# Projecting memory's keys and values first, three jobs with 512 columns, and other rules in the list schedule

## The chip, the cores and the metric

The kernel runs on one core of one Trainium2 chip. The metric is the device time of one execution in microseconds (us). Three runs of the kernel before took 517.40, 517.46 and 520.27 us, the median is 517.46. The profile is one further execution, which took 516.72 us, with a span of 514.9 us from its first to its last instruction.

## The reference

One decoder layer on 512 tokens of width 1024. Four groups of heads work side by side on one projection of the normed input, and their outputs, gated, go through one output projection:

```
h = RMSNorm_pre(x)
cols = h @ w_in       # q, k, v of four groups, and z
A: MoBA block attention, 8 heads x 64     B: NSA attention (compressed, selected, window), 8 heads x 64
C: retention, 4 heads, key 64, value 128
D: cross-attention into 256 memory tokens, 4 heads x 128; keys and values = RMSNorm(mem) @ w_mem_kv
o = concat(A, B, C, D) * silu(z)
out = x + RMSNorm_post(o @ w_out)
```

Everything is fp32. With 512 tokens, MoBA and the selected and window branches of NSA come down to causal attention over all tokens.

## The kernel before, in words

**Products.** Each fp32 operand is split into a high part H, which TensorE takes in its fast fp32r format, and a low part L = operand - H. A product is three matmuls, H·H, H·L and L·H. For the weights, a piece of 512 KB (128 partitions x 1024 columns) is loaded by SP's queue into a ring `wr` of two buffers, ScalarE casts it to H and GpSimd subtracts to get L, into a ring `w` of four buffers (`load_to`, `split_to`). The input's H and L lie transposed in `hH` and `hL`.

**Jobs.** A projection is cut into jobs of 256 columns of weights. `dim_job` puts the output's columns on the partitions and streams the tokens: 512 columns a matmul for x, 256 for memory (MK0, MK1). `tok_job` puts the tokens on the partitions and streams the weights, 256 columns a matmul (280 for NV): it is used where values are made, in BV0 and BV1 (MoBA), MV0 and MV1 (memory), RV0 and RV1 (retention), each over all tokens, 4 tiles of 128 or, for memory, 2. Results stand in PSUM banks with the tag G, of which there are three; S has four, U one. ScalarE and VectorE split each result into H and L again (`*_evac`).

**Two streams.** `g_stream` yields the projections in the order of the string ORDER (line 173), `a_stream` yields softmax attention (`softmax_stream`) and then retention (`ret_stream`). A loop at the end of `hybrid_kernel` mixes them: after each step it takes the stream that is behind, by PE time weighted with RATIO, which has one number for NSA, MoBA, memory and retention each. Tiles of 4 KB a partition, the slots `R`, hold what lives between jobs; there are 18, and a job waits for as many as it needs (`grab`). Letters in ORDER: Z and Y are pairs of gate columns (a Y stores its tiles to DRAM and they come back later), V, Q, C, R the projections, M and W memory's keys and values, x and m the loading and scaling of memory, which ride inside the next job. Memory's keys and values are made after MoBA's projections.

**The start.** x comes first. The norm and transposes of x, NV's weight splits and NV's matmuls are interleaved by hand in the string FIRST (line 178), and pinned: an instruction that is pinned stays behind the one recorded before it on its engine. Seven matmuls on zeros (WARM) run ahead and between.

**The order on each engine.** `Order` (line 184) records every instruction with a cost and what it depends on, and `run` plans a list schedule: for ScalarE and VectorE the one due first, with due times counted back from TensorE's recorded order; for GpSimd and SP the one recorded first (DUE). `fix` makes that order binding. A load counts 45 ns late and transfers cost 250 or 930 ns plus 1.32 to 1.47 ns per KB. Every recorded instruction carries line 360 in the profile, the line of the wrapper, so rows are told apart by tiles.

**The end.** `out_job` runs twice, for two halves of the output's columns. The first half starts when softmax attention is done; it takes the gated outputs of the four groups in OUT_ORDER, retention's last. The last token tile's second half has two banks of 256 columns, then come the last norm, the residual and the store (`finish`).

## Time and profile before

| | |
|---|---|
| median of 3 runs | 517.46 us |
| the profiled execution | 516.72 us |
| its span | 514.9 us |
| TensorE (PE) busy | 503.0 us, 98% |
| ScalarE (ACT) busy | 359.7 us, 70% |
| GpSimd (POOL) busy | 330.2 us, 64% |
| VectorE (DVE) busy | 329.2 us, 64% |
| DMA moved | 101.19 MB, mean 197 GB/s |

The page lists each engine's busy time, the span in 40 slices, the DMA queues, the chain of work that ended last and the costliest groups of instructions. A group's row says output tile, input tiles, shape and count, then busy time and the mean of one, then the idle time in front of it and what ended that. Matmuls are pipelined and their records overlap: the mean of one (393 ns for 512 columns) is longer than the distance between two.

### The profile page before, as it was taken

To read this page: it belongs to the slowest core of one execution; us is meant where nothing else is said; L and a number is where in the kernel's file an instruction comes from. 1 tells how busy PE (TensorE), PEld (TensorE's weight loads), DVE (VectorE), ACT (ScalarE), POOL (GpSimd) and SP (SyncE) were. 2 spreads that over 40 slices of the span, in tenths; PEclk is the share of its full clock that TensorE was granted. 3 is DMA by queue.
4 is the path that set the end of the run, shared out by engine and by line. 5 is a ranking of instruction groups with operands and counts; after the bars stand their busy time and mean duration, and the time that the engine had idled before them with its cause. 6 is when DMAs were issued, how large, how long until landed. Compare 5 with 4: busy or idle time off the path is not lost.

```text
span 514.9 us, 8572 instructions
## 1 busy us (share of the span) xinstructions
PE 503.0 (98%) x2730; PEld 433.8 (84%) x2730; DVE 329.2 (64%) x947; ACT 359.7 (70%) x810; POOL 330.2 (64%) x244
## 2 busy tenths in 40 slices
PE   8999999999999999999999999999998999989995
PEld 5988878788888998888998998988798888878884
DVE  6727378887879888768833786539884435772006
ACT  6557688977987889999967899746947655343202
POOL 4255646577666967777999758875937886264400
PEclk9999999999999999999999999999999999999999
DMA  8433458599579988875886299967792551341104
GB/s 313 166 101 106 133 162 273 150 305 281 164 253 295 262 246 246 252 216 189 240 268 193 96 310 288 273 245 234 244 288 84 181 174 54 122 158 59 71 0 163
DMA packets 42622, 101.19 MB, mean 197 GB/s; under 512 B 4561, under 2 KB 21713, under 8 KB 42578
## 3 DMA queue, kind: packets, MB, share of 16 engines
q1 hardware_dynamic: 42432, 100.58, 61.7%
q8 instruction: 21, 0.34, 0.3%
q14 instruction: 23, 0.19, 0.1%
q10 hardware_dynamic: 146, 0.08, 0.1%
HBM read 74.43 MB, written 26.21 MB: 195 GB/s over the span
## 4 chain that ended last, share of the span: by engine, by line
PE 71%; ACT 9%; DVE 9%; issue 4%; POOL 3%; DMA 3%; DVEq 0%; SPq 0%; ACTq 0%; POOLq 0%
PE bG L360 46%; PE bS L360 14%; PE bU L360 10%; ACT R L360 3%; DVE R L360 3%; ACT bS L360 3%; DVE bS L360 2%; DMA wr<-in_w 2%; POOL w L360 2%; ACT w L360 2%; DVE P L360 2%; DVE st L360 1%; ACT pt L360 1%; DMA x<-in_x 1%; DVE tb L360 1%
## 5 line engine op out<-in xcount | busy, mean ns | idle before, releaser
L360 POOL TENSOR_TENSOR w<-wr,w 128x1024 fp32r<-128x1024 f32 x76 | 182.9, 2409 | 104.3 <-ACT w L360 95.2
L360 PE MATMUL bG<-hH,w 128*128 128x512 f32 x640 | 210.0, 393 | 0.0
L360 PEld LDWEIGHTS bG<-hH,w 128*128 128x128 f32 x640 | 119.3, 188 | 23.1 <-POOL w L360 0.4
L360 PE MATMUL bG<-hL,w 128*128 128x512 f32 x320 | 125.5, 392 | 0.0
L360 POOL TENSOR_TENSOR pt<-pf,pt 128x384 fp32r<-128x384 f32 (+3 forms) x112 | 94.1, 858 | 40.7 <-ACT pt L360 40.5
L360 ACT ACTIVATE bS<-bS,st 128x256 f32<-128x256 f32 (+3 forms) x200 | 99.2, 515 | 22.1 <-DVE st L360 20.7
L360 ACT CAST w<-wr 128x1024 fp32r<-128x1024 f32 x76 | 80.0, 1053 | 42.4 <-DMA wr<-in_w 17.8
L360 PEld LDWEIGHTS bG<-hL,w 128*128 128x128 f32 x320 | 60.2, 188 | 10.6
L360 PE MATMUL bG<-w,hH 128*128 128x256 f32 (+1 forms) x304 | 62.1, 301 | 0.0
L360 PE MATMUL bS<-R,R 128*128 128x256 f32 (+4 forms) x280 | 60.6, 315 | 0.9 <-DVE chid L360 0.5
L360 DVE STREAM_TRANSPOSE tb<-bS 128x384 f32<-128x384 f32 (+3 forms) x112 | 54.7, 498 | 10.2 <-ACT bS L360 8.4
L360 PE MATMUL bU<-pt,R 128*128 128x512 f32 (+3 forms) x264 | 55.1, 326 | 1.5 <-POOL pt L360 1.3
L360 PEld LDWEIGHTS bS<-R,R 128*128 128x128 f32 x280 | 46.6, 189 | 9.3 <-DVE tb L360 1.9
L360 PEld LDWEIGHTS bU<-pt,R 128*128 128x128 f32 x264 | 45.0, 188 | 8.7 <-POOL pt L360 1.5
L360 ACT CAST pt<-pf 128x256 fp32r<-128x256 f32 (+3 forms) x112 | 48.2, 456 | 4.3 <-DMA pf<-pd 4.1
L360 PEld LDWEIGHTS bG<-w,hH 128*128 128x128 f32 x304 | 49.4, 190 | 2.0
L360 DVE TENSOR_REDUCE st<-bS 128x1 f32<-128x256 f32 (+2 forms) x88 | 45.2, 524 | 3.9 <-PE bS L360 3.5
L360 PE MATMUL bG<-w,hL 128*128 128x256 f32 (+1 forms) x152 | 44.4, 300 | 0.0
L360 DVE TENSOR_TENSOR bS<-bS,keep 128x128 f32<-128x128 f32 x88 | 25.3, 293 | 29.6 <-PE bS L360 29.1
L360 PE MATMUL bG<-w,R 128*128 128x256 f32 (+1 forms) x168 | 31.4, 331 | 0.0
L360 DVE TENSOR_TENSOR R<-bG,R 128x128 fp32r<-128x128 f32 (+3 forms) x43 | 18.1, 436 | 18.5 <-ACT R L360 11.2
L360 PEld LDWEIGHTS bG<-w,hL 128*128 128x128 f32 x152 | 28.9, 190 | 1.1
(145 smaller groups left out, 730.2 us busy)
## 6 DMA issues: line engine op xcount, KB each, us to landing
wr<-in_w SPq DMA_DIRECT2D x76, 512.0 KB, 3.6
pd<-tb SPq DMA_DIRECT2D x24, 640.0 KB, 4.4
pf<-pd SPq DMA_DIRECT2D x96, 160.0 KB, 4.3
zd<-R SPq DMA_DIRECT2D x8, 512.0 KB, 4.6
zb<-zd SPq DMA_DIRECT2D x8, 256.0 KB, 4.3
od<-zb SPq DMA_DIRECT2D x8, 256.0 KB, 3.2
R<-in_rtab SPq DMA_DIRECT2D x4, 512.0 KB, 6.1
R<-zd SPq DMA_DIRECT2D x4, 512.0 KB, 5.9
```

What stands on the lines that cost most here:

```text
L360: i = f(*args, **kw)
```

## The change

- MV, BV and RV become one job each of 512 columns (`wide_job`): weights come in four pieces of 512 KB with two k-tiles each, two token tiles are accumulated side by side in two G banks, and with four token tiles the same four split pieces are used in a second pass. RV's evacuation handles four heads at once.
- Memory's keys and values come before everything (`mem_first`): the columns of memory and the weights of MV are loaded first, in the order of LOADS, into eight raw buffers of their own. MV runs, then MK0 and MK1, and the norm and transposes of x ride inside these jobs (`x_chain`). Keys and values are stored to DRAM and the job M loads them back into four slots. Then NV runs as an ordinary job. FIRST and its pins are gone; nine warm-up matmuls run ahead. The first three pieces and memory's scaled columns get their low part from VectorE.
- The planner: GpSimd and SP go by due time too, a VectorE operation with two SBUF inputs and a GpSimd operation exclude each other, transfers cost 20 ns plus 2.5 or 3.25 ns per KB, a load counts 450 ns late, and the first matmuls cost double.
- Sizes: 20 slots instead of 18; a PSUM tag X of three for the start; retention accumulates in S banks instead of U; the second output half uses other banks; a transposed tile comes back one step earlier (LAGS); other ORDER (five Y instead of eight) and RATIO.

```diff
-    ("BV0", [_win("mv", 0, 256)]),
+    ("BV", [_win("mv")]),
...
-    ("MV0", [("w_mem", 512, 768)]), ("MV1", [("w_mem", 768, 1024)]),
+    ("MV", [("w_mem", 512, 1024)]),
...
-    ("RV0", [_win("rv", 0, 256)]), ("RV1", [_win("rv", 256, 512)]),
+    ("RV", [_win("rv")]),
...
-RET_BANK = "U"
+RET_BANK = "S"
 RET_LAG = 9
-SLOTS = 18
+SLOTS = 20
 PATIENCE = 60
-DUE = {'PE': 0, 'ACT': 1, 'DVE': 1, 'POOL': 0, 'SP': 0}
+DUE = {'PE': 0, 'ACT': 1, 'DVE': 1, 'POOL': 1, 'SP': 1}
 DUE_LAG = 1500
 WAIT = 120
 MARGIN = 600
 TABLE = 1283
-LATE = 45
+LATE = 450
 DMA_ISSUE = 352
-PS_BUFS = {"S": 4, "U": 1, "G": 3}
-BANKS = {"S": "S", "T": "S", "U": "U", "G": "G", "C": "S"}
-OUT_BANKS = ("GGGU", "SSTT")
-LAGS = (1, 1, 2, 3, 2, 1)
+PS_BUFS = {"S": 4, "U": 1, "G": 3, "X": 3}
+BANKS = {"S": "S", "T": "S", "U": "U", "G": "G", "C": "S", "X": "X"}
+OUT_BANKS = ("GGGU","SSSU")
+LAGS = (1, 1, 1, 3, 2, 1)
 D1, DW, DR, DH, NS, DV = LAGS
 FB, XB, ZB = 2, 2, 2
 PIN = ""
 MAN = ""
-ORDER = "s Y1 K p0 Y0 Y2 Y5 Y3 p1 Y6 V0 Q0 Q1 C0 x Y4 V1 Q2 m Q3 M1 M0 W0 C1 W1 RQ Y7 RK RV0 RV1"
-LAST_BANK = "U"
+ORDER = "s Y1 K p0 Y0 Z2 Y3 V Y5 p1 Q0 Y6 Q1 Z4 Q2 Q3 C0 M C1 Z7 RQ RK RV"
+LAST_BANK = "G"
 LAST_PARTS = ((0, 384), (384, 704), (704, 1024))
 LATER = 4000
-WARM = (4, 3)
-FIRST = ("g0 g1 w q0 r0 V0 V1 s00 t00 s01 t01 p0 d1 p2 p3 a00 a01 l00 l01 | | | | q1 V2 p4 d5 r1 V3 p6 s10 s11 d7 | | "
-         "t10 | t11 q2 a10 a11 l10 l11 | r2 q3 s20 s21 | | | | | | t20 | t21 r3 a20 a21 l20 l21 s30 s31 | W2 | | | | "
-         "t30 | | t31 | a30 a31 l30 l31 | | | | | | | | |")
-RATIO = (2.8, 4.92, 2.5, 2.09)
+WARM = 9
+FIRST_DVE = 3
+FIRST_RAW = 8
+LOADS = "c0 w c1 w c2 c3 w r0 w r1 x0 s w x1 w x2 w x3 w w w"
+XV, XK, XS, XE = 8, 6, 0, 2
+RATIO = (2, 2.61, 1.3, 1.2)
...
-            far = outs[0].space == bass.MemoryType.DRAM
             small = tuple(outs[0].shape)[0] == 32
-            op["cost"], op["dma"] = DMA_ISSUE, 870 if small else (930 if kb > 200 else 250) + kb * (1.32 if far else 1.47)
+            self.loads += 1
+            rate = 2.5 if outs[0].space == bass.MemoryType.DRAM or self.loads < 25 else 3.25
+            op["cost"], op["dma"] = DMA_ISSUE, 720 if small else 20 + kb * rate
         elif name == "PE":
             n = math.prod(tuple(outs[0].shape)[1:])
-            op["cost"] = max(108.5, 11 + 0.4246 * n)
+            op["cost"] = max(108.5, 11 + 0.4246 * n) * (2 if self.cold > 0 else 1)
+            self.cold -= 1
...
-                b = 1.6
+            elif name == "DVE" and fn != "tensor_scalar" and len(ins) > 1 and all(x.space != PSUM for x in ins):
+                op["lock"] = True
...
+                if e == "POOL":
+                    t = max(t, lock)
+                elif "lock" in ops[k]:
+                    t = max(t, free["POOL"])
...
+            if "lock" in o:
+                lock = t + o["lag"]
...
-            if j < 2:
-                late.append((H, L, w))
...
+            for c in parts_of(j, n):
+                ACT.copy(H[:, c], w[:, c])
+                (DVE if j < FIRST_DVE else POOL).tensor_tensor(L[:, c], w[:, c], H[:, c].bitcast(F32), op=ALU.subtract)
...
+    def mem_columns(k2):
+
+        mt = slot(mem_ids["x"][k2], [128, 2, 2, 256], F32R)
+        for k in range(2):
+            x, g = mem_x[k2][:, k], mem_g[:, 2 * k2 + k:2 * k2 + k + 1]
+            ACT.activation(mt[:, 0, k], x, AF.Copy, scale=g)
+            DVE.scalar_tensor_tensor(mt[:, 1, k], x, g, mt[:, 0, k].bitcast(F32), op0=ALU.mult, op1=ALU.subtract)
+            memT.append((mt[:, 0, k, :], mt[:, 1, k, :]))
...
+    def wide_job(name, cols, ntok, evac):
+
+        first = None
+        for t0 in range(0, ntok, 2):
+            ps = [bank("G") for _ in range(2)]
+            for pi in range(4):
+                if first is None or t0 == 0:
+                    wH, wL = piece(name, pi, min(2, 3 - pi) if ntok > 2 else 2)
+                    first = pindex[name, 0]
+                else:
+                    wH, wL = wt[first + pi]
+                    split_to(first + 3 + pi)
+                tks = [slice(128 * (t0 + m), 128 * (t0 + m) + 128) for m in range(2)]
+                for ms in ((0, 1),) if pi < 3 else ((0,), (1,)):
+                    for k in range(2):
+                        kt = 2 * pi + k
+                        H, L = cols(kt)
+                        c = slice(512 * k, 512 * k + 512)
+                        for x, (a, w) in enumerate(((H, wH), (L, wH), (H, wL))):
+                            for m in ms:
+                                mm(ps[m], a[:, tks[m]], w[:, c], kt == 0 and x == 0, kt == 7 and x == 2)
+                        yield 3 * len(ms) * cost(512)
+                    if pi == 3:
+                        evac(t0 + ms[0], ps[ms[0]])
+                        yield 0
+        split_to(first + 7)
+        later(name)
...
+            st = t_([128, 4], F32, "rst", 2)
+            DVE.tensor_reduce(st, ps.rearrange("p (a d) -> p a d", a=4), axis=AX.X, op=ALU.add)
+            ACT.activation(st, st, AF.Copy, scale=-1.0 / 128)
+            for a in range(4):
+                ACT.activation(rv[a][:, t, 0, :], ps[:, 128 * a:128 * a + 128], AF.Identity, bias=st[:, a:a + 1])
+            for a in range(4):
+                DVE.scalar_tensor_tensor(rv[a][:, t, 1, :], ps[:, 128 * a:128 * a + 128], st[:, a:a + 1],
+                                         rv[a][:, t, 0, :].bitcast(F32), op0=ALU.add, op1=ALU.subtract)
...
-        done.add("NV")
-        mx = mem_load(mraw)
+        yield from mem_first()
+        nid = yield from grab(2)
...
+        yield from tok_job("NV", h_cols, 4, 280, nevac)
...
+        def mem_back(ids):
+
+            mem_ids["kv"] = ids
+            for i, far in zip(ids, mem_far):
+                x = slot(i, [128, 2, 512], F32R)
+                dma("z", x.bitcast(F32), far)
+                n = len(mk) // 2
+                if len(mk) < 4:
+                    for m in range(2):
+                        mk[2 * n + m] = x[:, m].rearrange("p (a c) -> p a c", a=2)
+                else:
+                    mv[len(mv)] = x
+            done.update(("MV", "MK1"))
+            yield 0
 
...
-            "M0": (["MK0"], 1, lambda ids: mem_k(0, ids)),
...
+            "M": ([], 4, mem_back),
...
+    def x_load(t):
+        xt = t_([128, 1024], F32, "x", 4)
+        dma("p", xt, io["x"][128 * t:128 * t + 128, :])
+        xx.append(xt)
+    def x_scaled(t):
+        ACT.activation(slot(SLOTS - 2 - t % 2, [128, 1024], F32), xx[t], AF.Square, accum_out=st[:, 0:1])
+        ACT.activation(st[:, 2:3], st[:, 0:1], AF.Sqrt, bias=eps, scale=1.0 / D)
+        DVE.reciprocal(st[:, 3:4], st[:, 2:3])
+            x = xx[t][:, halves[c]]
+            DVE.scalar_tensor_tensor(x, x, st[:, 3:4], preg[c], op0=ALU.mult, op1=ALU.mult)
+    def x_turned(t, c):
+        p = bank("X")
+            PE.transpose(p[:, 128 * k:128 * k + 128], xx[t][:, 512 * c + 128 * k:512 * c + 128 * k + 128], ident)
+        p = p.rearrange("p (k q) -> p k q", k=4)
+        ACT.copy(hH[d], p)
+        DVE.tensor_tensor(hL[d], p, hH[d].bitcast(F32), op=ALU.subtract)
+    def x_chain():
+        for c in range(2):
+            norm_g(c)
+            yield 436
+        for t in range(4):
+            x_scaled(t)
+            yield 0
+            yield 0
+            for c in range(2):
+                x_turned(t, c)
+                yield 4 * 108
+    mem_far = []
+    def mem_away(i, tiles):
+        far = dram.tile([128, 2, 512], F32, name=f"mf{i}", tag=f"mf{i}", bufs=1)
+        dma("z", far, tiles.bitcast(F32))
+        mem_far.append(far)
+    def mem_first():
+        ids = yield from grab(13)
+        mem_ids.update(tmp=ids[0:2], x=ids[2:6], row=ids[10])
+        mvt = [slot(i, [128, 2, 512], F32R) for i in ids[6:8]]
+        mkt = []
+        n = 0
+        for what in LOADS.split():
+            if what == "w":
+                load_to(n)
+                n += 1
+            elif what == "s":
+                small_loads()
+            else:
+                {"c": mem_load, "r": lambda t: row_load(ids[11 + t]), "x": x_load}[what[0]](int(what[1]))
+        mem_columns(0)
+        split_to(0)
+        for k2 in range(1, 4):
+            mem_columns(k2)
+        free_later = ids[11:13]
+        def first_riders():
+            yield from mem_rstd()
+            yield from x_chain()
+        x = first_riders()
+        yield from ride(wide_job("MV", m_cols, 2, mv_evac(mvt)), rider_of(x, XV), 1, 1)
+        free.extend(free_later + mem_ids["tmp"])
+        for c in range(2):
+            i = ids[8 + c]
+            if c == 0:
+                yield from mem_row()
+            yield from ride(dim_job(f"MK{c}", m_cols, 256, mk_evac(2 * c, i)), rider_of(x, XK), XS, XE)
+            mkt.append(slot_of[i])
+        for i, t in enumerate(mkt + mvt):
+            mem_away(i, t)
+        mk.clear()
+        mv.clear()
+        yield from x
+        free.extend(mem_ids["x"] + [mem_ids["row"]] + ids[6:10])
...
+    nv_plan = ("MV", "MK0", "MK1", "NV", "NKVC")
```

## Rows read from the trace of the kernel before

**Rows 1.** The page: busy share of TensorE, and the landing of stored gates.
```profile
PE 503.0 (98%) x2730; PEld 433.8 (84%) x2730; DVE 329.2 (64%) x947; ACT 359.7 (70%) x810; POOL 330.2 (64%) x244
...
R<-zd SPq DMA_DIRECT2D x4, 512.0 KB, 5.9
```

**Rows 2.** The chain that ended last: start, length, what, count.
```profile
116.56 5.49 PE bG L360 x24
```

**Rows 3.** Windows: two of the start, two with 256-column matmuls only (MK, RV).
```profile
core 0: us, PE busy (x) PEld busy (x) DVE busy (x) ACT busy (x) POOL busy (x), PEclk, DMA share, GB/s
1.46:9.04 7.58, 7.44 (x20) 4.71 (x20) 4.82 (x11) 5.11 (x10) 3.07 (x4) 1.00 0.93 322
9.04:26.68 17.64, 16.94 (x122) 15.94 (x121) 12.15 (x28) 11.12 (x26) 4.53 (x4) 1.00 0.56 218
296.50:303.50 7.00, 7.00 (x61) 7.00 (x60) 5.78 (x25) 6.92 (x17) 3.32 (x2) 1.00 0.95 336
378.85:395.65 16.80, 16.80 (x142) 16.80 (x141) 11.37 (x31) 13.08 (x25) 5.90 (x4) 1.00 0.51 137
```

**Rows 4.** Timeline of the start: start, length, engine, operation, count, idle before.
```profile
1.46 2.07 PE L360 MATMUL bS<-P 128*128 128x512 f32 x4 [1.46 <-POOL P L360]
...
3.38 0.63 ACT L360 ACTIVATE R<-x 128x512 f32<-128x512 f32 x1 [0.19 <-DMA x<-in_x]
...
10.84 0.30 PE L360 MATMUL bG<-vh,hH 128*128 128x280 f32 x1
...
11.62 0.29 PE L360 MATMUL bG<-vh,hH 128*128 128x280 f32 x1
...
26.55 0.29 PE L360 MATMUL bG<-vh,hL 128*128 128x280 f32 x1
```

**Rows 5.** Windows from 20 to 500 us: three of seven, and the sum of all.
```profile
80.00:360.00 280.00, 279.79 (x1546) 243.90 (x1545) 206.52 (x669) 232.26 (x559) 207.75 (x161) 1.00 0.78 242
360.00:400.00 40.00, 38.26 (x255) 34.49 (x254) 29.00 (x78) 28.45 (x68) 27.13 (x25) 1.00 0.67 203
...
460.00:464.00 4.00, 2.51 (x14) 2.02 (x13) 1.96 (x3) 0.81 (x2) 3.54 (x3) 1.00 0.39 131
...
sum 480.00, PE 476.11 PEld 411.96 DVE 306.95 ACT 341.88 POOL 324.14; mean PE 68.02 PEld 58.85 DVE 43.85 ACT 48.84 POOL 46.31
```

**Rows 6.** Groups by shape, three engines: count, busy us, mean ns, idle before.
```profile
L360 ACT CAST w<-wr 128x1024 fp32r<-128x1024 f32 x76 | 80.0, 1053 | 42.4 <-DMA wr<-in_w 17.8 <-PE bU L360 13.7 <-PE bG L360 7.1
...
L360 ACT ACTIVATE R<-bG,rst 128x128 fp32r<-128x128 f32 x16 | 5.9, 373 | 6.6 <-DVE rst L360 6.5
...
L360 ACT CAST hH<-bS 128x512 fp32r<-128x512 f32 x8 | 4.7, 587 | 4.9 <-PE bS L360 4.9
L360 ACT ACTIVATE R<-R,keep 128x256 fp32r<-128x256 f32 x8 | 3.7, 506 | 1.6 <-PE bU L360 1.3 <-PE bS L360 0.2
L360 ACT ACTIVATE R<-x 128x1024 f32<-128x1024 f32 x3 | 3.2, 1061 | 0.0
...
L360 DVE TENSOR_REDUCE st<-bS 128x1 f32<-128x512 f32 x24 | 16.4, 682 | 0.1
...
L360 DVE SCALAR_TENSOR_TENSOR R<-bG,rst,R 128x128 fp32r<-128x128 f32 x16 | 5.1, 345 | 6.5 <-ACT R L360 6.3
...
L360 POOL TENSOR_TENSOR w<-wr,w 128x1024 fp32r<-128x1024 f32 x76 | 182.9, 2409 | 104.3 <-ACT w L360 95.2 <-PE bG L360 4.3 <-PE bS L360 4.2
```

**Rows 7.** DMA of the first 14 us: rate in 40 slices, and bytes.
```profile
GB/s 0 0 0 0 12 193 351 259 273 306 224 123 277 331 357 351 388 376 399 400 403 380 422 409 407 424 410 421 421 433 410 372 369 429 433 434 398 433 421 433
DMA packets 1812, 4.51 MB, mean 322 GB/s; under 512 B 193, under 2 KB 577, under 8 KB 1812
```

**Rows 8.** Timeline: two VectorE subtracts with two SBUF inputs, and a late matmul.
```profile
11.47 0.45 DVE L360 TENSOR_TENSOR vl<-vr,vh 128x280 fp32r<-128x280 f32 x1 [0.91 <-ACT vh L360]
...
68.42 2.06 DVE L360 TENSOR_TENSOR P<-small,P 128x192 fp32r<-128x192 f32 x1
...
71.01 0.69 PE L360 MATMUL bS<-R,R 128*128 128x512 f32 x2 [0.45 <-DVE chid L360]
```

**Rows 9.** Timeline: the output projection behind retention's last head.
```profile
462.14 0.70 PE L360 MATMUL bS<-w,hH 128*128 128x512 f32 x2 [1.49 <-DVE R L360]
```

More of the change, by code (lines that the diff above doesn't have):

```diff
@@ L192, in __init__ @@
         self.tc, self.ops, self.seen, self.tags = tc, [], {}, {}
-        self.last = {}
+        self.last, self.cold, self.loads = {}, WARM, 0
     def engine(self, eng, name):
@@ L256, in record @@
                 a = 140
-            elif name == "DVE" and len(ins) > 1 and all(x.space != PSUM for x in ins):
-                b = 1.6
+            elif name == "DVE" and fn != "tensor_scalar" and len(ins) > 1 and all(x.space != PSUM for x in ins):
+                op["lock"] = True
             op["lag"] = a + b * n + (190 if kw.get("accum_out") is not None else 0)
@@ L456, in hybrid_kernel, with small_loads @@
     DVE.memset(eps4, 4.0 * EPS)
+    def small_loads():
+        SP.dma_start(first, io["first"])
+        SP.dma_start(small, io["small"])
+        SP.dma_start(consts, io["consts"])
     plist, pindex = [], {}
@@ L466, in plan @@
                 plist.append((name, i))
-    raw, wt, late = {}, {}, []
+    raw, wt = {}, {}
     def pin(i):
@@ L474, in hybrid_kernel, with parts_of @@
     state = {"load": 0, "split": 0}
+    def parts_of(j, n):
+        return [slice(a, a + 512) for a in range(0, n, 512)] if j == 0 else [slice(0, n)]
     def load_to(i):
@@ L536, in row_rstd @@
     def row_rstd(xt, junk, st):
-        pin(ACT.activation(junk, xt, AF.Square, accum_out=st[:, 0:1]))
+        ACT.activation(junk, xt, AF.Square, accum_out=st[:, 0:1])
         ACT.activation(st[:, 1:2], st[:, 0:1], AF.Sqrt, bias=eps, scale=1.0 / D)
@@ L560, in mem_row @@
     def mem_row():
-        row = bank("C")
+        row = bank("X")
         parts = []
@@ L1321, in ret_stream @@
     def ret_stream():
-        yield from need("RV1", "SR")
+        yield from need("RV", "SR")
         for p in (4, 5):
@@ L1422, in z_job, with bv @@
                 done.add("S" + grp)
-        def bv(c, ids):
+        def bv(ids):
             vs, evac = v_evac(ids)
-            for a in range(2):
-                vtiles["b", 2 * c + a] = vs[a]
-                moba_ids[2 * c + a] = [ids[a]]
-            yield from tok_job(f"BV{c}", h_cols, 4, 256, evac)
+            for a in range(4):
+                vtiles["b", a] = vs[a]
+                moba_ids[a] = [ids[a]]
+            yield from wide_job("BV", h_cols, 4, evac)
         def bqk(p, ids):
@@ L1626, in hybrid_kernel, with rider_of @@
+    def rider_of(gen, n):
+        for _ in range(n):
+            y = next(gen, None)
+            if y is None:
+                return
+            yield y
+    nv_plan = ("MV", "MK0", "MK1", "NV", "NKVC")
+    for name in nv_plan:
+        plan(name)
     plan("NQ0", "CMPK")
     plan("NKQ0", "CMPV")
+    ACT.dma_start(mem_g, io["mem_g"])
     ACT.dma_start(grow[0].bitcast(F32), io["pre_g"])
-    ACT.dma_start(first, io["first"])
-    pin(ACT.activation(ssy[:, 0, 0:1], eps, AF.Sqrt))
+    ACT.activation(ssy[:, 0, 0:1], eps, AF.Sqrt)
@@ L1633, in hybrid_kernel @@
     POOL.memset(wu.bitcast(F32), 0.0)
-    for t in range(4):
-        xt = t_([128, 1024], F32, "x", 4)
-        for c in halves if t == 0 else (slice(0, 1024),):
-            dma("p", xt[:, c], io["x"][128 * t:128 * t + 128, c])
-        xx.append(xt)
-        if t < 2:
-            load_to(t)
-    SP.dma_start(small, io["small"])
-    SP.dma_start(consts, io["consts"])
-    mraw = [free.pop(0), free.pop(0)]
-    split_to(1)
-    wps = bank("S")
-    def warm(n):
-        for _ in range(n):
-            pin(mm(wps, wu[:, 0:128], wu, True, True))
-    warm(WARM[0])
-    nid = [free.pop(0), free.pop(0)]
-    vs, nevac = nv_evac(nid)
-    vtiles["n", 0], vtiles["n", 1] = vs
-    nsa_ids["v"] = nid
-    nv = [tok_tile("NV", h_cols, t, 280, nevac, 0) for t in range(4)]
-    def nv_step():
-        nv_count[0] += 1
-        next(nv[0])
-        if nv_count[0] % 8 == 0:
-            for _ in nv.pop(0):
-                pass
-    nv_count = [0]
-    for x in FIRST.split():
-        n = int(x[1:] or 0)
-        if x == "|":
-            nv_step()
-        elif x[0] in "pd":
-            first_low(POOL if x[0] == "p" else DVE, n)
-        elif x == "w":
-            warm(WARM[1])
-        elif x[0] == "W":
-            split_to(n)
-        elif x[0] in "stal":
-            {"s": scaled, "t": turned, "a": high, "l": low}[x[0]](n // 10, n % 10)
-        else:
-            {"g": norm_g, "q": squares, "r": root, "V": first_high}[x[0]](n)
+    wps = bank("X")
+    for _ in range(WARM):
+        mm(wps, wu[:, 0:128], wu, True, True)
     streams = {"g": g_stream(), "a": a_stream()}
```

210 lines of the change are left out of this document (61 added, 149 removed).

## The prediction

> **What bounds the kernel now.** I read the page first [rows 1]: TensorE is busy 98% of the span and no other engine passes 70%. So the question for every edit is whether it takes columns off TensorE, or shortens a stretch in which TensorE does nothing useful. Matmul records overlap, so the busy share hides gaps; I then took the pace of matmuls from counts over time: 24 matmuls of 512 columns in 5.49 us, 0.229 each [rows 2], and 256-column runs at 7.00 us for 59 (two of the 61 only touch the window's edges), 0.119 each, and 16.80 us for 140, 0.120 [rows 3]. Time that is not matmuls at this pace lies in the start, in a few places of the middle, and in the tail behind the last matmul.
>
> The **start** [rows 4]: the first matmul comes at 1.46, and the first job (NV, 96 matmuls of 280 columns) ends at 26.68. The useful work up to there is 96 x 0.130 (six matmuls from 10.84 to 11.62), 32 transposes at about 0.11 (a 128-column matmul can't cost more than the 256-column pace) and 4 x 0.229 for the norm row: 16.9 us, so 9.8 us are lost. Part of this is the low clock: the first four 512-column matmuls take 2.07 us together, about 0.43 each where 0.229 is the later pace, the 1.2 GHz level against 2.4; NV runs at the higher level from 10.84 on. The clock column says 1.00 for the whole stretch; the paces contradict it. The **middle** [rows 5]: from 20 to 500 us TensorE is idle 480 - 476.11 = 3.9 us, of which 1.74 between 360 and 400 and 1.49 at 460 to 464.
>
> **The change, part by part.**
>
> *512-column jobs.* BV, MV and RV had 192 + 96 + 192 = 480 matmuls of 256 columns and get 240 of 512. A pair costs 0.238 to 0.240, one wide matmul 0.229 [rows 2, 3]: 240 x 0.009 to 0.011 = 2.2 to 2.6 us. TensorE is full where these stand, so this counts wholly. I take 2.6, as the nearest job (RV, the 16.80 us window) runs at 0.120. The split weights of BV and RV are used twice from the same four buffers, so no load is added, but in the first pass a piece lasts only 12 x 0.229 = 2.75 us against 2.41 on GpSimd [rows 6]; attention's matmuls stretch that, and I cost it at nothing. *New wait:* a wide job takes two of the three G banks, and its second pair needs a bank of the first. RV's evacuation is a reduce (0.68), a small activation (some 0.3), four activations of 0.373 and a last subtract of 0.345, 2.8 us [rows 6], against 7 matmuls = 1.6 us of cover: 1.2 us, once inside RV and once before the output projection, 2.4 if no retention or attention matmul fills it. I expect it filled: 0, with 2.4 as the far end. BV's evacuation has no reduce and fits.
>
> *Memory first.* The work up to NV's end becomes 16.9 + MV's 48 x 0.229 = 11.0 + MK's 96 x 0.119 = 11.4 + 0.4 for the row of norms = 39.7 us, and what counts is the time lost on top, against 9.8. Nine warm-up matmuls at 0.43 end at 5.3. The first 256 KB had landed by 3.38 (the first Square), and the first weight half and its cast have come by 5.4, an estimate from the next 256 KB and half of the 1.05 us cast. So useful work begins 5.4 us in: a bound of 5.4 lost, 4.4 gained. Then the feed. The queues moved 0.40 to 0.43 MB/us once full, 4.51 MB in the first 14 us [rows 7]. In the order of LOADS, MV's last piece is complete at 3.7 MB, about 12.0 us, and MK's first at 5.6 MB, about 16.7; each needs a cast of 1.05, a GpSimd subtract of 2.41 [rows 6] and some 0.3 of semaphores. MV's last quarter then starts at 15.8 and ends at 18.5, 2.1 later than unstarved. MK starts at 20.5, 2.0 later still, of which the transposes of the first tile of x and the norm row fill about 1.5. After that a piece lasts 2.9 us on TensorE and 2.41 on GpSimd, and nothing waits. That is 5.4 + 2.1 + 0.5 = 8.0 lost. SP now issues by due time, and MV's last piece is due before a row of memory that only the norms need; with 1.2 us (512 KB) less wait, 6.8. I take 7.5: **2.3 us gained.** On the other side stands a clock that stays low to 10.84 as before, 2.7 us, mostly under the same waits.
>
> *The round trip.* Keys and values go out (4 x 512 KB) and come back for attention, and three of eight gate pairs no longer do: 2 MB more and 1.5 MB less each way. Memory's 4 MB of weights leave the stretch of 80 to 360, where the DMA share is 0.78, for the start [rows 5]. The stored gates land in 5.9 us [rows 1]. With SP issuing a job ahead of attention's need this is hidden, 0; if SP is stuck behind them, one landing, 5.9, as the softmax transfers queue behind.
>
> *The list schedule.* At 68.42 a VectorE subtract with two SBUF inputs took 2.06 us for 192 columns while GpSimd worked, where one of 280 columns took 0.45; `chid` came late behind it and TensorE stood still for 0.45 [rows 8]. The new model places such work around GpSimd; I count 0.4 back. The Trainium skill (SBUF — State Buffer, Who interferes with whom) says that such a pair of operations excludes each other for a whole instruction; the trace agrees at this place (2.06 against 0.45). By that rule the start's eight memory columns and three weight pieces on VectorE could be held up too, each by one GpSimd subtract; GpSimd's first piece there comes only after them, so the sum stays. The 1.49 at 460 is the output projection waiting for retention's last normalization [rows 9]; the ratio for that stretch goes from 2.09 to 1.2 in attention's favour and retention gets other banks than the single U. I count it as gone. Of the 1.74 at 360 to 400, nothing. Middle, rounded: **2.0 us**, between 3.9 and, with RV's banks, -2.4.
>
> The tail (last norm, last store) is untouched.
>
> **Sum:** 2.6 + 2.3 + 2.0 = 6.9 us. The profiled execution took 516.72, 0.74 less than the median of 517.46; the saving is taken from the median: **510.6 us**.
>
> **Rivals.**
>
> *Only the columns come back.* The feed loses in the start what the early beginning wins (9.8 lost as before), and other waits take the place of those in the middle: 517.5 - 2.6 = 515, between 513.5 and 518.5. For it: TensorE is busy in 279.79 of 280 us between 80 and 360, so no schedule can win there; against it: the 1.49 us wait has a plain cause, which the change moves. A clock that stays at its lower level while MV comes in bursts is part of it: 48 matmuls at 0.43 cost 9.7 us more, 3.5 of them under the waits for weights, 6 us on the start.
>
> *Everything comes back.* Start lost 5.4, middle idle 0: 2.6 + 4.4 + 3.9 = 10.9, so 506.6.
>
> *Slower: ScalarE paces the start.* Up to NV's end ScalarE has 8 casts of 1.053 and NV's two of about 1.2, eight activations of 0.506, six squares of 1.06 and eight casts of 0.587, 26 us [rows 6], and by my estimate 11 of roots, sums, evacuations and the next job's casts: 37 us from 3.4 on. They must fit before 39.7 + 9.8 = 49.5 for the start to cost no more than before, and before 54.1 (2.6 + 2.0 later) for the kernel to be no slower. The point is a ScalarE busy for 37 of 50.7 us, 73%. In the start of before it was busy 5.11 of 7.58 and 11.12 of 17.64 us [rows 3], about 65%; at that share it ends at 60.3, 6.2 over, and the time is 517.5 + 6.2 = 524, between 519 and 528. Against it: it had little to do then, and it held 232.26 of 280 us, 83%, in the middle [rows 5].
>
> *The change does not do what it says:* if wide matmuls run no faster than 0.239, the 2.6 are missing, and the time is that of the first rival or near it.
>
> **Chances.** Forecast (507.5 to 513.5) 0.48; only the columns 0.27; everything 0.12; slower 0.13. A difference of 1%, 5.2 us, is about what a measurement of this kernel can tell from none: faster means below 512.3. Nearly nine tenths of the forecast's case and all of the third make 0.54 faster; the slower case is over 522.6 in about 0.10; 0.36 remain. The range of 505 to 518 leaves out the slower case and the ends of the others.
>
> **What would show it.** Wide matmuls: 240 fewer in all, at 0.229. The start: NV ending near 47 (39.7 + 7.5); over 49.5 early memory has cost time, over 54 the whole change has. Idle time in front of MV's and MK's matmuls and its releasers tell whether loads, casts or subtracts were late. The middle: no wait for retention's normalization in the output projection, no long VectorE subtract before `chid`. RV's banks: idle TensorE beside a reduce of 512 columns. Wrong altogether if the start alone moves the time by over 5 us either way.

## The result and the profile after

The changed kernel takes 511.85 us (511.2 to 512.67), the kernel before 517.43 us beside it: a ratio of 0.9883, 95% interval [0.9843, 0.9922]. The medians are 5.6 us apart, the means, of which the ratio is made, 6.1. The profiled execution took 511.8 us with a span of 510.02, against 516.72 and 514.91 before, so the traces have 4.9 us to account for.

The page of the changed kernel, to be held against [rows 1], and its DMA groups (issues, size of each, median us to landing): TensorE has 238 matmuls fewer (240 fewer, and two more warm-ups), and keys and values go out and come back with landings like those of the stored gates.

```profile
PE 498.1 (98%) x2492; PEld 418.5 (82%) x2492; DVE 337.2 (66%) x940; ACT 358.7 (70%) x808; POOL 312.6 (61%) x226
...
mf<-R SPq DMA_DIRECT2D x4, 512.0 KB, 6.0
R<-mf SPq DMA_DIRECT2D x4, 512.0 KB, 4.6
```

The timeline of the changed kernel's start (start, length, engine, operation, count, idle before), to be held against [rows 4]:

```profile
1.31 4.21 PE L368 MATMUL bX<-P 128*128 128x512 f32 x9 [1.31 <-POOL P L368]
...
5.68 0.91 ACT L368 ACTIVATE R<-R,mem_g 128x256 fp32r<-128x256 f32 x2 [1.32 <-DMA R<-in_memT]
...
6.24 4.56 PE L368 MATMUL bG<-w,R 128*128 128x512 f32 x16 [0.72 <-ACT R L368]
11.21 2.12 PE L368 MATMUL bG<-w,R 128*128 128x512 f32 x8 [0.40 <-DVE w L368]
13.25 0.73 PE L368 MATMUL bS<-R,ones 1*128 1x512 f32 x2
...
13.32 5.23 POOL L368 TENSOR_TENSOR w<-wf,w 128x1024 fp32r<-128x1024 f32 x2 [11.92 <-ACT w L368]
...
15.03 3.81 DVE L368 SCALAR_TENSOR_TENSOR R<-R,mem_g,R 128x256 fp32r<-128x256 f32 x2 [1.29 <-ACT R L368]
...
18.89 2.11 PE L368 MATMUL bG<-w,R 128*128 128x512 f32 x8 [0.21 <-DVE R L368]
20.84 1.96 PE L368 MATMUL bG<-R,w 128*128 128x256 f32 x15
...
27.96 0.64 PE L368 MATMUL bX<-P,ones 128*128 128x128 f32 x4
...
48.72 0.29 PE L368 MATMUL bG<-vh,hL 128*128 128x280 f32 x1
```

MV begins at 6.24, MK at 20.84, and NV's last matmul gives way to the next job at 48.85. Useful work up to there is the 39.7 us of the prediction, so 9.1 us are lost, 0.7 less than before.

Windows of the changed kernel (us, then busy time and count of each engine, clock, DMA share, rate), to be held against [rows 5], the last row being the sum from 20 to 500 us:

```profile
80.00:360.00 280.00, 277.65 (x1365) 233.09 (x1364) 212.28 (x703) 238.85 (x581) 191.61 (x149) 1.00 0.75 231
360.00:400.00 40.00, 39.10 (x170) 31.26 (x169) 29.22 (x52) 23.78 (x47) 25.14 (x26) 1.00 0.53 172
460.00:464.00 4.00, 4.00 (x20) 3.34 (x19) 2.00 (x7) 2.73 (x9) 0.00 (x0) 1.00 0.26 105
...
sum 480.00, PE 476.67 PEld 403.56 DVE 318.63 ACT 342.03 POOL 306.49; mean PE 158.89 PEld 134.52 DVE 106.21 ACT 114.01 POOL 102.16
```

The wait at 460 is gone and half of that between 360 and 400, but 80 to 360 us, where TensorE had stood still for 0.21 us, now has 2.35 of idle time. The largest single wait there is at 280.36, behind softmax loads that took 8.01 us where 4.4 is the median; SP had issued two of memory's four returning loads right ahead of them (the chain of waits, then the timeline of SP and TensorE):

```profile
270.11 8.01 DMA pf<-pd
```

```profile
266.77 1.63 SPq L368 DMA_DIRECT2D R<-mf  x2
268.50 2.07 SPq L368 DMA_DIRECT2D pf<-pd  x4
...
280.36 0.73 PE L368 MATMUL bS<-R,R 128*128 128x512 f32 x2 [0.73 <-DVE tb L368]
```

The balance of the traces: every matmul's distance to the next one, less the pace of its width from [rows 2, 3], is time lost; another choice of pace moves all these sums by some tenths, and their differences less. The last matmul begins at 503.88 us instead of 508.89, 5.0 earlier, and this splits into 2.6 for the columns, 0.7 for the start and 1.6 for the middle (8.1 lost from 20 to 500 before, 6.4 now; in busy time the middle shows less, 3.89 idle and 3.33). The tail behind it is 6.1 in both.

### The profile page after: what moved, and what is told of

Read it like the earlier page. It is cut to its first block, busy times and chain, and to the rows that moved or that the text cites. A ratio compares the mean times of both kernels' runs of the same rounds, so it can differ in the third digit from the quotient of the medians.

```text
span 510.0 us, 8055 instructions
## 1 busy us (share of the span) xinstructions
PE 498.1 (98%) x2492; PEld 418.5 (82%) x2492; DVE 337.2 (66%) x940; ACT 358.7 (70%) x808; POOL 312.6 (61%) x226
## 4 chain that ended last, share of the span: by engine, by line
PE 78%; DMA 7%; DVE 6%; ACT 5%; issue 2%; SPq 1%; POOL 0%; DVEq 0%; ACTq 0%
PE bG L368 52%; PE bS L368 16%; PE bU L368 9%; DMA pf<-pd 3%; DMA pd<-tb 2%; DVE R L368 2%; DVE P L368 2%; DMA wf<-in_w 2%; ACT R L368 1%; ACT bS L368 1%; ACT pt L368 1%; DVE tb L368 1%; DMA R<-in_memT 1%; SPq L368 1%; PE bX L368 1%
## 5 line engine op out<-in xcount | busy, mean ns | idle before, releaser
L368 POOL TENSOR_TENSOR w<-wr,w 128x1024 fp32r<-128x1024 f32 x68 | 163.6, 2409 | 98.1 <-ACT w L368 88.6
L368 POOL TENSOR_TENSOR pt<-pf,pt 128x256 fp32r<-128x256 f32 (+2 forms) x112 | 94.4, 857 | 41.0 <-ACT pt L368 39.5
L368 PE MATMUL bG<-w,hH 128*128 128x512 f32 (+1 forms) x192 | 57.1, 382 | 0.1
L368 PEld LDWEIGHTS bS<-R,R 128*128 128x128 f32 x280 | 47.2, 188 | 11.5 <-DVE tb L368 2.4
L368 ACT CAST pt<-pf 128x256 fp32r<-128x256 f32 (+2 forms) x112 | 48.1, 452 | 11.4 <-DMA pf<-pd 9.6
L368 PE MATMUL bU<-pt,R 128*128 128x512 f32 (+1 forms) x216 | 44.6, 327 | 1.6 <-ACT pt L368 1.5
L368 PEld LDWEIGHTS bG<-w,hH 128*128 128x128 f32 x192 | 35.2, 188 | 7.0 <-ACT hH L368 0.5
L368 PE MATMUL bG<-w,R 128*128 128x512 f32 (+1 forms) x144 | 35.4, 380 | 1.4 <-ACT R L368 0.7
L368 DVE TENSOR_TENSOR R<-bS,R 128x512 f32<-128x512 f32 (+4 forms) x20 | 11.7, 586 | 37.5 <-ACT P L368 33.0
L368 DVE TENSOR_TENSOR R<-bG,R 128x128 fp32r<-128x128 f32 (+4 forms) x44 | 18.5, 433 | 24.4 <-ACT R L368 18.8
L368 PE MATMUL bG<-w,hL 128*128 128x512 f32 (+1 forms) x96 | 34.5, 381 | 0.0
```

The costliest lines, as they stand in the source:

```text
L368: i = f(*args, **kw)
```

## Experiments

Ratios are to the kernel before on the same chip in the same runs, with 95% intervals. Each trace is of one execution, and executions of one kernel can lie several us apart here, so a difference between two traces is not yet one between two kernels. "Lost" is used as in the balance above; the changed kernel lost 12.0 us in all, 5.6 of them up to 40 us, the kernel before 14.7 and 6.6.

**One part of the change at a time.** Into the kernel before, the bank alone:

```
-RET_BANK = "U"
+RET_BANK = "S"
```

> The kernel before with one edit: retention accumulates in S banks instead of the single U bank. Theory (the wait of 1.49 us of the output projection at 460 came from the ratio of the two streams, the banks have little to do with it): 517.4, within 0.5 us, and the wait stays. Rival (the single bank held retention back): the wait goes, 515.9.

516.58 us, 0.9979 [0.9959, 0.9999]. The wait at 460 went (1.8 us lost between 460 and 480 before, 0.5 here), as the rival had it, though in its trace (519.04, next to the longest of ten executions) more than that came up elsewhere, the longest new one 2.0 us at 253 behind a VectorE operation.

The wide jobs alone, under the old order and planner:

```
 RET_BANK = "S"
-    ("BV0", ...), ("BV1", ...), ("MV0", ...), ("MV1", ...), ("RV0", ...), ("RV1", ...)
+    ("BV", [_win("mv")]), ("MV", [("w_mem", 512, 1024)]), ("RV", [_win("rv")])
+    def wide_job(name, cols, ntok, evac): ...
```

> The kernel before with retention in S banks, and BV, MV and RV as one 512-column job each; memory stays where it was, the planner too. Theory: 240 matmuls fewer, and the sum of matmuls at their pace falls by 2.6 us against the run with the S banks alone: 514.8 if that stands at 517.4. Rival (RV's longer evacuation holds its G bank, 1.2 us twice): 2.4 of the 2.6 us come back as idle TensorE beside the 512-column reduce, 517.2.

519.53 us, 1.0034 [1.001, 1.0058]: above even the rival's 517.2, but not by the rival's cause. The 2.6 us of columns are there in the count of matmuls, but the kernel loses 19.9 us where it had lost 14.7. No wait stands where RV does, whose reduces lie between 393 and 408: TensorE is busy for all of 360 to 460 (the last window below). The longest wait is MK's, for memory columns that GpSimd still makes in this kernel, among pieces of weights, softmax and gates (timeline):

```profile
295.22 1.83 POOL L360 TENSOR_SCALAR R<-R,keep 128x256 f32<-128x256 f32 x2
...
297.01 1.26 POOL L360 TENSOR_TENSOR zb<-zb,o 128x512 f32<-128x512 f32 x1
...
298.23 1.26 POOL L360 TENSOR_TENSOR R<-R,R 128x512 fp32r<-128x512 f32 x1
...
299.55 1.86 PE L360 MATMUL bG<-R,w 128*128 128x256 f32 x7 [2.92 <-POOL R L360]
```

```profile
360.00:460.00 100.00, 100.00 (x466) 82.60 (x465) 57.87 (x119) 59.66 (x120) 70.65 (x51) 1.00 0.52 160
```

The four planner rules alone, in the kernel before (exclusion, prices of transfers, due times for SP and GpSimd, lateness):

```
-DUE = {'PE': 0, 'ACT': 1, 'DVE': 1, 'POOL': 0, 'SP': 0}
+DUE = {'PE': 0, 'ACT': 1, 'DVE': 1, 'POOL': 1, 'SP': 1}
-LATE = 45
+LATE = 450
-... 870 if small else (930 if kb > 200 else 250) + kb * (1.32 if far else 1.47)
+... 720 if small else 20 + kb * rate
-                b = 1.6
+                op["lock"] = True
```

> The kernel before with the four planner rules of the change alone (the exclusion of VectorE and GpSimd, the new prices of transfers, SP and GpSimd ordered by due time with 450 instead of 45 for lateness); the order of the work, the narrow jobs, the banks and the start stay as they were. The changed kernel without these rules kept a ratio of 0.9944 to before, with them 0.9883. Theory (the rules are worth something wherever the list of work is long enough to choose from, also without early memory): 514 to 516, with the 0.45 us wait at 71 us gone. Rival (the rules only pay for what early memory asks of the start, where there are eight pieces of weights, memory's columns and the norms to put in order): 516.5 to 518.5, as before. Second rival (the old order of work and the ratios were made for the old rules, so the new ones open new waits): above 519.

522.7 us, 1.0111 [1.0088, 1.0134]: slower, the second rival. The start is as before (7.0 lost up to 40 us), the wait at 460 is still there (1.48 at 467.94), and new ones lie between 60 and 80 and between 320 and 400 us, where TensorE is busy for 76.77 of 80 us instead of 78.26. The wait for `chid` at 71 is gone, as the theory had it, but waits for other things took its place: 2.2 us are lost from 60 to 80, 1.4 before.

```profile
320.00:400.00 80.00, 76.77 (x444) 66.51 (x443) 51.77 (x129) 54.22 (x120) 54.70 (x41) 1.00 0.72 225
```

**The changed kernel without the rules.** All four undone, the order of work, early memory and wide jobs kept:

```
-DUE = {'PE': 0, 'ACT': 1, 'DVE': 1, 'POOL': 1, 'SP': 1}
+DUE = {'PE': 0, 'ACT': 1, 'DVE': 1, 'POOL': 0, 'SP': 0}
-LATE = 450
+LATE = 45
(and the old prices of transfers, and b = 1.6 for the lock)
```

> The changed kernel with the planner's old rules: no exclusion of VectorE and GpSimd, the old costs of transfers, a load 45 ns late, GpSimd and SP in recorded order. Theory (TensorE is idle for only 3.3 us between 20 and 500 us, so a planner can win little there, and the start is set by what arrives when): 511.9 to 514, most of the loss in the start, where SP would then issue memory's rows ahead of MV's last weights. Rival (memory first works only with these rules): 516 or more.

516.8 us, 0.9944 [0.9908, 0.998]: the rival by its number, though the kernel stays faster than the kernel before, so early memory works without the rules too, only less well. Its ten executions lie between 512.10 and 520.22 us, four of them under 514.3, and the profiled one took 518.21, so the trace is of one of the longer ones. There the start is what fails: NV ends at 56.27, 7.4 us later than with the rules, and 12.9 us are lost up to 40 us. MV comes in short runs with waits between them and runs its first 26 matmuls, up to 20.9 us, at 0.43 each, the lower level of 1.2 GHz; then MK waits for GpSimd:

```profile
8.38 0.79 PE L368 MATMUL bS<-R,ones 1*128 1x512 f32 x1
9.10 2.93 PE L368 MATMUL bG<-w,R 128*128 128x512 f32 x6
...
16.68 9.63 PE L368 MATMUL bG<-w,R 128*128 128x512 f32 x32
...
29.55 0.61 PE L368 MATMUL bG<-R,w 128*128 128x256 f32 x3 [1.69 <-POOL w L368]
```

The exclusion rule alone undone:

```
-                op["lock"] = True
+                b = 1.6
```

> The changed kernel without the one rule that a VectorE operation with two SBUF inputs and a GpSimd operation exclude each other. Theory: the rule is worth the 0.4 us of one late chid and a little in the start, 512.3. Rival (it is worth more, as VectorE and GpSimd meet over a hundred times): 513.5 or more. Third: nothing, 511.9, since other orders are as good.

518.27 us, 0.9985 [0.9959, 1.0011], by its number the rival. The start loses 9.4 us instead of 5.6, NV ends at 52.55, 3.7 later. Two rows show a part that the rule had kept away: without it the norm row's subtract stands behind a pair of memory columns that GpSimd's subtracts hold up, and TensorE waits for it; in the changed kernel it is done from 8.22 us, before GpSimd begins.

```profile
13.17 5.13 POOL L368 TENSOR_TENSOR w<-wf,w 128x1024 fp32r<-128x1024 f32 x2 [11.77 <-ACT w L368]
...
15.01 3.58 DVE L368 SCALAR_TENSOR_TENSOR R<-R,mem_g,R 128x256 fp32r<-128x256 f32 x2 [1.52 <-ACT R L368]
18.51 1.27 DVE L368 TENSOR_TENSOR R<-R,R 1x512 fp32r<-1x512 f32 x2
...
19.23 0.50 PE L368 MATMUL bS<-R,ones 1*128 1x512 f32 x1 [1.40 <-DVE R L368]
```

The clock has a larger part. In this start the granted clock was 0.50, the lower level, in two stretches where the changed kernel kept the higher one; half of these 6.8 us, 3.4, is lost by it, while MV's waits take no more than there. The first stretch lies ahead of GpSimd's first subtract, so no hold-up by GpSimd made it; ahead of it TensorE had stood idle for 1.78 us after the nine warm-ups, waiting for a cast (0.72 in the changed kernel). First the timeline, then the windows:

```profile
6.89 5.08 PE L368 MATMUL bG<-w,R 128*128 128x512 f32 x14 [1.78 <-ACT w L368]
```

```profile
7.90:11.30 3.40, 3.40 (x9) 2.64 (x8) 2.66 (x5) 3.17 (x5) 0.00 (x0) 0.50 1.04 408
21.60:25.00 3.40, 3.40 (x11) 2.73 (x10) 2.05 (x4) 2.05 (x4) 2.44 (x2) 0.50 1.02 410
```

1.7 us more are lost at 130 us, where the granted clock fell a third time (last section). Of the ten executions, nine had a mean granted clock of 0.987 to 0.992 and took 516.49 to 522.85 us; the tenth had 0.999 and took 513.97. How much of the cost is the exclusion by itself is therefore open. That one rule undone costs more than all four is not shown either, as the two intervals overlap.

**The start.** Memory's first columns issued ahead of the first half of a weight piece:

```
-        if kind in PIN:
+        if kind in PIN or 1 < order.loads < 5:
```

> The changed kernel with SP's first issues held in the order of the list of loads, so that the first 256 KB of memory's columns go ahead of the first half weight piece, which went first in the changed kernel by its due time. There the first memory columns landed at 5.68 us and the first useful matmul came at 6.24, where the prediction had 5.4. Theory (the start waits for the first columns, everything behind them for a feed that is limited by the queues' bytes): the first useful matmul comes near 5.4, but MV's last quarter and MK stand as late as before, NV ends within 0.3 us of 48.85, and the time is 511.5 to 512.2. Rival (what the start loses at its beginning it keeps): NV ends near 48.0, and the time is 511.0.

512.95 us, 0.9907 [0.9875, 0.994]; neither. The columns are there 0.28 us earlier, but then the weights are late: the first useful matmul comes at 6.87 and waits for ScalarE's cast of a weight, and NV ends at 49.45. Both are needed first, and they share the queues.

```profile
6.87 2.36 PE L368 MATMUL bG<-w,R 128*128 128x512 f32 x9 [1.35 <-ACT w L368]
```

Four of MV's pieces on VectorE:

```
-FIRST_DVE = 3
+FIRST_DVE = 4
```

> The changed kernel with four instead of three of MV's weight pieces subtracted on VectorE, so that GpSimd's first subtract in the start is MK's. In the changed kernel two operations of VectorE on memory's last columns took 3.81 us for two beside a GpSimd subtract of MV's last piece (5.23 for two), and MV's last quarter began at 18.89, released by VectorE. Theory (this exclusion is why MV's last quarter came 3 us later than the 15.8 of the prediction): the last quarter begins at 16.5 to 17.5, NV ends 0.5 to 1.5 us earlier than 48.85, and the time is 510.5 to 511.4. Rival (the queues' bytes set MK's beginning, at 20.84, whatever MV does): the last quarter is earlier, MK begins where it did, NV ends within 0.3 us of 48.85, and the time is 511.6 to 512.1.

513.22 us, 0.9904 [0.9869, 0.9939], above both ranges; the trace (of the shortest of four executions, 511.53) decides for the rival. The hold-up shrinks (2.77 us for the two columns, and MV's last 18 matmuls run through), yet MK begins at 20.69 and NV ends at 48.86.

```profile
16.49 4.36 PE L368 MATMUL bG<-w,R 128*128 128x512 f32 x18
```

The expectation misread one row: at 18.89 the changed kernel's MV had only eight of its 48 matmuls left, inside its last quarter, which had begun at 17.61, 1.8 us later than the prediction's 15.8. Here it begins at 17.97, no earlier: MV as a whole is late, not its last quarter.

Four warm-up matmuls instead of nine:

```
-WARM = 9
+WARM = 4
```

> The changed kernel with four warm-up matmuls instead of nine, so that TensorE is idle from about 3 to 6.2 us. Theory (what TensorE did before MV decides the granted clock in it, and the warm-up pays for itself): MV's first matmuls run at the lower level, 0.43 us each against 0.229, for some 4 us, which costs up to 2 us where MV doesn't wait for weights anyway; NV ends near 50, and the time is 512.5 to 514. Rival (MV waits for its feed, so a low clock there is hidden): MK begins where it did, NV ends within 0.3 us of 48.85, and the time is 511.6 to 512.1.

513.97 us, 0.9934 [0.991, 0.9958]; the theory. MV's first matmuls run at 0.43 us each up to 12.3 us, and NV ends at 50.59, 1.74 later (the trace is of the longest of nine executions, 516.5):

```profile
1.31 2.07 PE L368 MATMUL bX<-P 128*128 128x512 f32 x4 [1.31 <-POOL P L368]
...
6.48 1.22 PE L368 MATMUL bG<-w,R 128*128 128x512 f32 x2 [1.63 <-ACT R L368]
7.63 0.79 PE L368 MATMUL bU<-R,ones 1*128 1x512 f32 x1
8.35 4.96 PE L368 MATMUL bG<-w,R 128*128 128x512 f32 x12
```

The rival has a case of its own, though. In the kernel without the trip to DRAM (below), with the same nine warm-ups as the changed one, MV's first nine matmuls ran at 0.44 each as well, from 6.42 to 10.42, and NV ended at 49.07, only 0.2 later: there the waits for the feed hid the low clock.

```profile
6.42 5.80 PE L368 MATMUL bG<-w,R 128*128 128x512 f32 x16 [0.90 <-ACT R L368]
```

**The middle.** Retention's bank and ratio put back:

```
-RET_BANK = "S"
+RET_BANK = "U"
-RATIO = (2, 2.61, 1.3, 1.2)
+RATIO = (2, 2.61, 1.3, 2.09)
```

> The changed kernel with retention's bank back on the single U and the last ratio back at 2.09. With the bank alone put into the kernel before, the 1.49 us wait at 460 had gone and the time was 0.2% lower. Theory (one bank for retention's products is what made the output projection wait): a wait of 1 to 1.5 us behind retention's last normalization comes back near 456 us, and the time is 1 to 1.5 us above the changed kernel's, 512.8 to 513.4. Rival (the new order of work has room there): no such wait, 511.8.

513.95 us, 0.9936 [0.9914, 0.9959]; the theory, 0.6 above its range: the wait is back, as in [rows 9]. Some 1.9 us more are lost from 320 to 420 us, too. As both edits were undone together, the share of each is not shown here.

```profile
461.27 0.70 PE L368 MATMUL bS<-w,hH 128*128 128x512 f32 x2 [1.57 <-DVE R L368]
```

Keys and values kept in slots, no trip to DRAM:

```
-            "M": ([], 4, mem_back),
-ORDER = "... Q3 C0 M C1 Z7 ..."
+ORDER = "... Q3 C0 C1 Z7 ..."
+        mem_ids["kv"] = ids[6:10]
```

> The changed kernel with memory's keys and values kept in their slots from the start until attention, so that the four transfers of 512 KB out and the four back are gone; four of the twenty slots are then taken all the time. Theory (the trip costs nothing by itself; the waits at 279 to 290 us of the changed kernel are queueing that other transfers would cause too): 511 to 513, and TensorE's gaps over 0.15 us between 270 and 300 stay or move. Rival (the returning keys and values stand in front of the softmax transfers on SP's queue, which took 8.0 us there where 4.3 is the median): the gaps at 279 to 290 go, and the time is 1 to 2 us lower, 510 to 511. Second rival (four slots fewer for the gates make new waits in the middle): 514 or more.

541.26 us, 1.0439 [1.0393, 1.0486]: the second rival, far beyond its bound. The waits at 279 to 290 are gone (0.4 lost from 260 to 300, 2.3 in the changed kernel), but the jobs that should lie beside attention don't come, and it runs alone from 363 to 395 (window). The granted clock is 0.70 there, so a part of the 26 us is the clock's. That the four slots are the reason is inferred from the edit, not shown.

```profile
360.00:400.00 40.00, 24.59 (x92) 19.70 (x92) 32.70 (x107) 28.36 (x87) 16.28 (x19) 0.70 0.72 217
```

The return put one job earlier, so that its loads go singly between the softmax's:

```
-ORDER = "... Q2 Q3 C0 M C1 Z7 ..."
+ORDER = "... Q2 Q3 M C0 C1 Z7 ..."
```

> The changed kernel with the return of memory's keys and values put one job earlier in the list of work, ahead of the first memory query job; SP then issues the four loads singly between the softmax transfers, where the changed kernel issues two of them right ahead of four softmax loads at 268.5 us, which took 8.0 us. Theory (those two loads are what made the softmax loads late, so the round trip costs what TensorE waits at 279 to 290, 1.9 us in three gaps): these gaps go or halve, and the time is 1 to 2 us lower, 510 to 511. Rival (the waits there are attention's own chain of softmax, DRAM and cast, which the schedule can only move): the excess between 260 and 300 stays at 2 us or comes up elsewhere, 511.5 to 513.

513.3 us, 0.9927 [0.9906, 0.9948]; the rival, 0.3 above its range. The place was right: from 260 to 300 us TensorE stands still for 0.01 us instead of 1.40 (windows of this kernel, then of the changed one). But 141 and 382 us have new waits of 0.8 and 2.0, and the kernel loses 12.4 us in all, against 12.0.

```profile
260.00:300.00 40.00, 39.99 (x190) 32.89 (x189) 26.88 (x81) 35.82 (x79) 30.07 (x27) 1.00 0.88 274
```

```profile
260.00:300.00 40.00, 38.60 (x183) 31.57 (x182) 25.93 (x80) 34.19 (x75) 28.08 (x23) 1.00 0.88 271
```

Eighteen slots:

```
-SLOTS = 20
+SLOTS = 18
```

> The changed kernel with 18 slots, as before, instead of 20. The order of TensorE's work is the same up to the first softmax products of attention's later heads and differs behind them, where a job must wait for slots that attention gives back. Theory (keys and values have been in DRAM while the slots were scarce, so two fewer cost little): 511.5 to 513. Rival (with slots short the jobs that should cover attention come late, as in the kernel that kept keys and values in four slots, where attention ran uncovered from 363 to 398 and lost 26 us): 516 or more, with the gaps between 340 and 400.

513.9 us, 0.9944 [0.992, 0.9967], between the two. The gaps are where the rival had them (6.4 us lost from 320 to 420, 3.1 in the changed kernel), but small.

No variant is shown to beat the changed kernel. The six that differ from it by a small edit and keep its rules (all but the one without the trip) measured 0.9904 to 0.9944, a little above its 0.9883, and all their intervals overlap with its own: which of them costs something is read from the points in their traces, not from the times.

Early memory with the old order of work was not run, nor the new ORDER, the other ratios, LAGS and the output's banks by themselves. So the experiments don't share out the gain among the edits.

## Why the prediction was right, point by point

**The columns: right in size.** 240 matmuls fewer, and wide ones at 0.226 to 0.236 us from start to start in MV where no wait lies between them. The stretch with RV runs without a gap from 381.9 to 400.9, 83 matmuls at 0.232 on average, so the banks cost nothing there and the far end of 2.4 did not come.

```profile
381.90:400.90 19.00, 19.00 (x82) 15.40 (x83) 8.30 (x18) 11.34 (x25) 10.37 (x12) 1.00 0.32 110
```

What I left out is the condition: the wide jobs alone gave the 2.6 back with 1.8 more, by waits elsewhere. That it "counts wholly" did not hold in the old order of work.

**The start: right in sign, too large.** 2.3 expected, 0.7 found; NV ended at 48.85, not 47.2. Term by term, against the 8.0 that the terms add up to: useful work began at 6.24 instead of 5.4, as memory's columns landed behind a weight piece (0.8 worse); the four matmuls of x's norm row cost 1.31 us on TensorE (13.25 to 13.91 and 15.48 to 16.13), where 4 x 0.229 was counted (0.4 worse); waits in MV took 2.3, where 2.1 was counted (0.2 worse); from MK on 0.2 was lost instead of 0.5 (0.3 better). That makes 9.1. The 7.5 had 0.5 less for SP's issue by due time, and that did not come. Memory's row of norms, the 0.4, is four matmuls of 128 columns at 27.96. The order of issue that I had called a bound, 5.4, can't be had by moving the columns forward alone, since the weights are then late. The feared low clock did not come in this trace: MV ran at the higher level from its first quarter. Nine warm-up matmuls don't ensure that: with the same nine, MV began at the lower level in the kernel without the trip and in the one with the old planner, and fell to it from 7.90 to 11.30 in the one without the exclusion.

The prediction said that GpSimd's first piece in the start comes only after VectorE's memory columns. That is wrong: GpSimd began at 13.32, and VectorE's last two columns took 3.81 us instead of 0.48 each (as the one at 13.27 took). The Trainium skill (SBUF — State Buffer, Who interferes with whom) says that the order of issue decides which of the two is held, and for a whole instruction; the trace agrees, as the pair got free when GpSimd's second subtract ended at 18.55. On TensorE's path it cost 0.37 us ahead of MV's last eight matmuls, and taking it away did not move NV's end.

**The round trip: 0 by itself, as predicted,** but not as hidden as I held it. Two returning loads stood in front of softmax loads, and 1.4 us of TensorE went there; with the loads issued singly the same time came up elsewhere, so the kernel's time does not show it.

**The middle: 2.0 expected, 1.6 found, with other parts.** The wait at 460 went, by the bank and the ratio, as the kernel with both put back shows. But the idle time between 80 and 360 rose from 0.21 to 2.35. I had written that no schedule can win there; it can lose there, and I gave that no term. The 0.4 for `chid` came back, but not by the rule that it was credited to: nothing waits for `chid` in the trace of the changed kernel without that rule, either.

**The planner: the mis-sized term.** I credited 0.4 us to the rules, for one late `chid`. By the ratios, undoing all of them in the changed kernel costs 3.2 us (0.9944 against 0.9883, though the two intervals overlap a little), and the start loses 7.3 more in its trace, of a long execution; undoing the exclusion alone costs 5.3, but its trace loses 3.4 by the clock in the start and 1.7 by the clock at 130 us. Yet put into the kernel before, the same rules cost 5.7. They are not a term that can be added to the others: what they do depends on the order of work that they arrange. The sum came out near the measured time, 510.6 against 511.85, because columns, start and middle each stood for the whole of their stretch, whichever edit made it. Some of the nearness is luck: 6.9 us were forecast and the traces have 4.9, the start alone 1.6 too few, but the medians lie 0.7 further apart than the profiled executions.

**The rivals.** "Only the columns come back", 515, lies outside the interval of 4.0 to 8.1 us saved, but its account of the middle (other waits take the place of those that go) is half of what happened. "Everything comes back" lies outside too: start and middle still lose 9.1 and 6.4. ScalarE did not pace the start; it was busy for 36.48 of the first 50 us, 73%, the very share that the prediction named as the point, and still MK and NV ran through, so the share alone does not decide it. That wide matmuls run no faster fell with their pace.

## What to carry to other kernels

In a kernel whose order is computed, no edit has a price of its own: each re-deals every wait, and here two parts of a change that were slower by themselves (1.0034 and 1.0111) belong to a whole, with early memory and another order of work, that was faster (0.9883). Price an edit by the stretch in which the work stands, with a term for new waits in stretches that are full now, and don't price a planner's rule by the one late instruction in the old trace: here another order of work removed that one without the rule. Before a difference between two traces is put down to an edit, compare their granted clocks.

## What the runs showed that was not expected

The granted clock can fall in the middle of a full kernel, and it need not fall in the next one. The same run of sixteen 64-column matmuls with one wide one between them is followed by the higher level in the changed kernel (seven wide matmuls in 1.15 us) and by the lower one in the kernel without the exclusion rule (seven in 1.74, then 0.43 each to 134.2). First the changed kernel's timeline, then the other's, then the other's windows, with the granted clock in the third column from the right:

```profile
125.49 1.20 PE L368 MATMUL bS<-R,R 128*128 128x64 f32 x10
...
126.84 1.15 PE L368 MATMUL bU<-pt,R 128*128 128x512 f32 x7
```

```profile
129.14 1.20 PE L368 MATMUL bS<-R,R 128*128 128x64 f32 x10
...
130.49 1.74 PE L368 MATMUL bU<-pt,R 128*128 128x512 f32 x7
```

```profile
127.00:130.50 3.50, 3.06 (x22) 2.44 (x21) 3.00 (x11) 3.50 (x10) 1.60 (x2) 1.00 0.21 86
130.50:132.00 1.50, 1.50 (x8) 1.46 (x7) 1.14 (x5) 1.50 (x4) 1.50 (x2) 0.60 0.95 300
132.00:134.20 2.20, 2.20 (x7) 1.78 (x7) 1.64 (x5) 1.51 (x3) 2.20 (x2) 0.50 0.97 235
```

It fell at the same place with four warm-ups (128.58, seven in 1.98), and there a second time behind a wait of 2.2 us at 283, for 3.4 us:

```profile
285.60:289.00 3.40, 3.30 (x8) 2.62 (x9) 3.09 (x12) 3.33 (x10) 1.82 (x2) 0.50 1.01 274
```

Two other long waits told of above were followed by the lower level as well: the 2.0 us at 253 in the kernel with the bank alone (254.1 to 257.5) and the 2.9 at 299 in the one with the wide jobs alone (299.4 to 302.8), so these waits cost more than their own length. The wait at 382 in the kernel with the early return, 1.8 us of idle time, was not. What decides it at one and the same sequence was not tried and stays open; it costs 1.6 to 1.8 us each time, as much as most of the effects looked for here.
